# Gate matrices of a 512-token PEER layer: three parts instead of two, products one step behind, candidate sums on ScalarE

## The chip, the cores and the metric

The kernel runs on one core of one Trainium2 chip. The metric is the device time of one execution in microseconds (us): the median of the runs before is 2933.96 us. The engines are called as in the profile: PE is TensorE, DVE is VectorE, ACT is ScalarE, POOL is GpSimd, SP is SyncE, which here issues the plain loads.

## What is computed

The program runs two transformer blocks over 512 tokens of width 1024. The change touches the last stage alone, the PEER layer of the second block, cut here to what matters (8 heads, 128 keys per half, 16 kept):

```python
q = (ht @ peer_wq).reshape(T, PEER_HEADS, PEER_DK)
s1 = jnp.einsum("thd,hnd->thn", q[..., :half], peer_k1)
s2 = jnp.einsum("thd,hnd->thn", q[..., half:], peer_k2)
v1, i1 = lax.top_k(s1, PEER_TOPK)
v2, i2 = lax.top_k(s2, PEER_TOPK)
cand = v1[..., :, None] + v2[..., None, :]        # 16 x 16 sums
sc, pos = lax.top_k(cand, PEER_TOPK)
experts = e1 * PEER_NKEYS + e2                    # of 16384
gates = jax.nn.softmax(sc, axis=-1)
a = jax.nn.gelu(jnp.einsum("ckd,cd->ck", peer_u[experts], h)) * gates
out = jnp.einsum("ck,ckd->cd", a, peer_v[experts])
```

Each token so uses 128 of 16384 rows of peer_u and of peer_v.

## The kernel before, in words

All of it stands in the function peer (lines 1462 to 1903). The scores are made in four passes over peer_wq (lines 1641 to 1666), whose weights are split on ACT and POOL for PE (`split`, line 83: the fp32r copy hi). `halves` takes the top 16 of each half on DVE; `best` (line 1541) takes four heads of 128 tokens: it makes the 50 sums of pairs that can be among the 16 largest into the tile cd (lines 1553 to 1557, nine additions on DVE over four heads at once), takes the top 16 of each head (lines 1558 to 1567), and turns positions into expert numbers with one-hots. It is called eight times. Four calls for the first 256 tokens lie in the passes; four for the last 256 tokens are drawn from the generator `picks`, a piece at a time, beside the tiles below. cd and most of its neighbours have one buffer each.

The first 256 tokens are done by **gathering**. `dots` (line 1786) gathers for each of 128 choices the peer_u rows of 128 tokens by an indirect DMA from POOL (line 1784) and takes the dot product with the token on DVE (line 1791): 128 for the first 128 tokens, then 128 for the next. When 128 are done, `factors` makes the gelus; `v_sum` (line 1805) takes four gathered peer_v tiles at a time through PE (line 1812), 16 matmuls: a row product, R0 to R31 for the first 128 tokens and R32 to R63 for the next. The peer_u gathers of the second 128 tokens lie between R0 and R31, four per row product. All gathers share twelve buffers (line 1781), so a gather waits until a dot or a row product has freed one.

The last 256 tokens are done **densely**. `u_tile` (U0 to U127 below) multiplies 128 experts by the 256 tokens on PE (line 1726, 16 matmul records a tile) and ACT writes the gelu into a slot of big (line 1728), which has 96 slots. `gates` builds the matrix of gate values from one-hots: for a batch of 8 tokens DVE makes the one-hot o2 of the lower expert digit (128 wide), the one-hot eq of the upper digit for the tiles n0 to n1 of a part, and its product with the gate in two halves, og (lines 1742 to 1748); PE multiplies them (line 1752, 16 fp16 matmuls of as many columns as the part has tiles: one product, G below), and DVE multiplies the result into big (line 1756). 32 batches make a part. `v_tile` (V0 to V127) then multiplies slot n by its peer_v tile (line 1763).

The order of the work is a list written by hand (lines 1861 to 1867): U0 to U95, V0, U96, V1, U97 and so on to U127, V32, then V33 to V127. Batches G are drawn beside these steps at an even rate: the first part (64 tiles) after U63 until V0 and the second (64 tiles) after U127 until V64. `fill` (line 1850) draws gathers: after each step as many units as its rate says, 1.4 until V0 and 2.4 from then on (line 1898), where a dot counts 1 and four peer_v rows count 4. A scheduler then sets each engine's order, and engines work their own queue strictly in that order. PSUM tiles come in three groups: pu (two buffers, U tiles and the second part's products), pw (four, the first part's products until V0, then the sums of the V tiles), pr (two, row products).

Of the kernel before, what the change touches and what calls it, by code (L numbers as in the profile page):

```python
# [31 lines left out]
class Kern:  # L32
# [1430 lines left out]
    def peer(self):  # L1463
# [2 lines left out]
        act = nc.scalar.activation  # L1466
        GT, DT, DW = (0, 1), (2, 3), 256
        NS, NA = 96, 52
        parts = [0, 64, 128]
        first = dict(zip([p - 1 for p in parts[1:]], parts))  # L1470
        TB = 8
        GS = 32768.0
        with ExitStack() as ctx:
# [68 lines left out]
            def best(t, h0):  # L1542

                H = slice(h0, h0 + NH)
                xf = wk.tile([128, NH, 2, 16], F16, tag="xf", name=self.nm("xf"))
                nc.vector.tensor_copy(xf[:], ix[t][:, H])

                xe = wk.tile([128, 2, 16, NH, 16], F16, tag="xe", name=self.nm("xe"))
                for i in range(2):
                    act(xe[:, i], xf[:, :, i, :].rearrange("p h v -> p v h")[:, :, :, None].to_broadcast([128, 16, NH, 16]),  # L1550
                        AF.Copy)
                cd = wk.tile([128, NH, NC], F32, tag="cd", name=self.nm("cd"))
                o, s = 0, v[t][:, H]
                for i, n in enumerate(pairs):
                    tt(cd[:, :, o:o + n], s[:, :, 1, 0:n], s[:, :, 0, i:i + 1].to_broadcast([128, NH, n]), op=OP.add)
                    o += n
                tt(cd[:, :, o:o + 8], s[:, :, 0, 8:16], s[:, :, 1, 0:1].to_broadcast([128, NH, 8]), op=OP.add)
                pi = wk.tile([128, NH, 16], U32, tag="pi", name=self.nm("pi"))
                for i in range(NH):
                    h = h0 + i  # L1560
                    r = wk.tile([128, NC], F32, tag="mr2", name=self.nm("mr2"), bufs=2)
                    nc.vector.max(sc[t][:, h, 0:8], cd[:, i, :])
                    nc.vector.match_replace(r[:], sc[t][:, h, 0:8], cd[:, i, :], -3e38)
                    nc.vector.max(sc[t][:, h, 8:16], r[:])
                    nc.vector.max_index(pi[:, i, 0:8], sc[t][:, h, 0:8], cd[:, i, :])
                    nc.vector.max_index(pi[:, i, 8:16], sc[t][:, h, 8:16], r[:])
                yield

                pf = wk.tile([128, SL], F16, tag="pf", name=self.nm("pf"))
                nc.vector.tensor_copy(pf[:], flat(pi[:]))  # L1570
                cm = wk.tile([128, 2, 7, SL], F16, tag="cm", name=self.nm("cm"))
                cs = wk.tile([128, 2, 3, SL], F16, tag="cs", name=self.nm("cs"))
                ij = wk.tile([128, 2, SL], F16, tag="ij", name=self.nm("ij"))
                mx = wk.tile([128, SL], F16, tag="mx", name=self.nm("mx"))
                tt(cm[:, 0], cut[:, 0], pf[:, None, :].to_broadcast([128, 7, SL]), op=OP.is_le)
                tt(cm[:, 1], cm[:, 0], cut[:, 1], op=OP.mult)
                ts(mx[:], pf[:], -41.0, 0.0, op0=OP.add, op1=OP.max)
                tt(cs[:], cm[:, :, 0:3], cm[:, :, 3:6], op=OP.add)
                tt(cs[:, :, 0], cs[:, :, 0], cm[:, :, 6], op=OP.add)
                tt(cs[:, :, 1], cs[:, :, 1], cs[:, :, 2], op=OP.add)  # L1580
                tt(cs[:, :, 0], cs[:, :, 0], cs[:, :, 1], op=OP.add)
                tt(ij[:, 0], cs[:, 0, 0], mx[:], op=OP.add)
                tt(mx[:], pf[:], cs[:, 1, 0], op=OP.subtract)
                stt(ij[:, 1], pf[:], 42.0, mx[:], op0=OP.is_lt, op1=OP.mult)

                oh = wk.tile([128, 2, 16, SL], F16, tag="oh", name=self.nm("oh"))
                for i in range(2):
                    tt(oh[:, i], i16[:], ij[:, i, None, :].to_broadcast([128, 16, SL]), op=OP.is_equal)
                tt(oh[:], oh[:], xe[:].rearrange("p a v h k -> p a v (h k)"), op=OP.mult)
                for w in (8, 4, 2):  # L1590
                    tt(oh[:, :, 0:w], oh[:, :, 0:w], oh[:, :, w:2 * w], op=OP.add)
                e = e12[t][:, :, H, :].rearrange("p a h k -> p a (h k)")
                tt(e, oh[:, :, 0], oh[:, :, 1], op=OP.add)
                if t in GT:
                    stt(e[:, 0], e[:, 0], 128.0, e[:, 1], op0=OP.mult, op1=OP.add)
                    nc.vector.tensor_copy(ei[t][:, 16 * h0:16 * h0 + SL], e[:, 0])
# [134 lines left out]
            def gates(n0, n1, psum):  # L1731


                w, g = n1 - n0, TB // 2

                def by2(x, t0, w):
                    return x[:, t0:t0 + TB].rearrange("p (g i) -> p g i", i=2)[:, :, None, :].to_broadcast([128, g, w, 2])

                for t0 in range(0, DW, TB):
                    o2 = ga.tile([128, g, 128, 2], F16, tag="o2", name=self.nm("o2"), bufs=2)  # L1740
                    eq = ga.tile([128, g, w, 2], F16, tag="eq", name=self.nm("eq"))
                    tt(o2[:], io[:, None].to_broadcast([128, g, 128, 2]), by2(e2b, t0, 128), op=OP.is_equal)
                    tt(eq[:], io[:, None, n0:n1].to_broadcast([128, g, w, 2]), by2(e1b, t0, w), op=OP.is_equal)
                    og = []
                    for j in range(2):
                        o = ga.tile([128, g, w, 2], F16, tag=f"og{j}", name=self.nm("og"), bufs=2)
                        tt(o[:], eq[:], by2(gp[j], t0, w), op=OP.mult)
                        og.append(o)
                    p = psum([128, TB, w])
                    for i in range(TB):  # L1750
                        for j in range(2):
                            nc.tensor.matmul(p[:, i, :], o2[:, i // 2, :, i % 2], og[j][:, i // 2, :, i % 2], start=j == 0,
                                             stop=j == 1)
                    for n, m, b, i in slots(n0, n1):
                        b = b[:, i:i + m - n, t0:t0 + TB]
                        stt(b, p[:, :, n - n0:m - n0].rearrange("p t n -> p n t"), 1.0 / GS, b, op0=OP.mult, op1=OP.mult)  # L1756
                    yield

            def v_tile(n, acc):
                raw = load(A["peer_v_2"][n * 128:n * 128 + 128, :], [D])  # L1760
# [90 lines left out]
            def fill(n):  # L1851
                with tc.issue_after(self.pace.ins):
                    while n > 0:
                        k = next(units, None)
                        if k is None:
                            return 0.0
                        n -= k
                return n
# [4 lines left out]
            for n in range(128):  # L1863
                while u < 128 and u < n + NS:
                    seq.append(("u", u))
                    u += 1
                seq.append(("v", n))
            acc, gt, todo, room = None, None, 0, 0.0
            nbatch = DW // TB

            for j, (kind, n) in enumerate(seq):
                if kind == "v" and n == 0:
                    acc = [[pw() for _ in range(2)] for _ in range(2)]
                if kind == "v" and n in parts and gt is not None:
                    for _ in gt:
                        pass
                    gt = None
                if kind == "u":
                    if n == NA:
                        for _ in picks:  # L1880
                            pass
                        rest_of_big()
                    if n % 3:
                        next(picks, None)
                    u_tile(n)
                else:
                    v_tile(n, acc)
                if gt is not None:
                    todo += rate
                    while todo >= 1:  # L1890
                        todo -= 1
                        next(gt, None)
                if kind == "u" and n in first:
                    if gt is not None:
                        for _ in gt:
                            pass
                    gt, todo = gates(first[n], n + 1, pw if first[n] == 0 else pu), 0.0

                    rest = sum(1 for x in seq[j + 1:seq.index(("v", first[n]))])
                    rate = nbatch / max(rest - 1, 1)  # L1900

                room = fill(room + (1.4 if acc is None else 2.4))
            while next(units, None) is not None:
                pass
            for t in DT:
# [87 lines left out]
```

## Time and profile before

| | us |
|---|---|
| runs | 2929.74, 2933.96, 2935.29 |
| median of the runs | 2933.96 |
| profiled execution, device time | 2927.91 |
| profiled execution, span from first to last instruction | 2926.2 |
| busy: PE, DVE, ACT, POOL | 2709.7, 1817.2, 1020.4, 724.4 |

The span is the time between the first and last instruction of one profiled execution; some 1.7 us lie around it. A busy share is a mean over the whole program, while the stage in question runs from about 1640 us to the end, and its stretches differ. A row of the timeline gives the start, the duration, the operation with its output and inputs, and in brackets how long the engine stood idle before it and what ended the wait. A row of a group gives busy time and mean duration, and the idle time before its instructions.

### The profile page before, as it was taken

Reading aid. Unit: us, or ns where it says so; the run is one execution under the profiler, and the core shown is the slowest. Engines: PE = TensorE matmul, PEld = TensorE weight load, DVE = VectorE, ACT = ScalarE, POOL = GpSimd, SP = SyncE. Lnnn points to the kernel's source line nnn. Section 1 sums busy time; section 2 is a strip of 40 time slices with the busy share of each in tenths; the row PEclk is TensorE's granted clock in tenths of the full one; section 3 lists DMA queues with packets and bytes.
Section 4 is the critical chain, followed back from the end, with each engine's and each line's share of the span. In section 5 each row is a group of like instructions: output and inputs, shape, how many; then the busy total and the mean of one; then the engine's idle time right before and its main releaser. Section 6 shows DMA issues by size and latency. Waiting matters only on the chain.

```text
span 2926.2 us, 37189 instructions
## 1 busy us (share of the span) xinstructions
PE 2709.7 (93%) x13218; PEld 1891.9 (65%) x13218; DVE 1817.2 (62%) x3747; ACT 1020.4 (35%) x1672; POOL 724.4 (25%) x679
## 2 busy tenths in 40 slices
PE   7999969999999879999999889996999887989998
PEld 5776757777777667766778778886855443433333
DVE  5562569998888858998535399968632224761001
ACT  5442348777777653345533332210100000000000
POOL 1000050000000110101000343575045445444443
PEclk9999979999999989999999999998999888999999
DMA  7226568989999843322222347899499999999998
GB/s 259 87 84 215 208 209 323 354 320 353 350 351 347 326 146 88 102 76 69 86 91 97 119 166 276 334 409 404 159 334 371 335 349 333 335 323 405 395 383 308
DMA packets 228684, 752.03 MB, mean 257 GB/s; under 512 B 28160, under 2 KB 28448, under 8 KB 228496
## 3 DMA queue, kind: packets, MB, share of 16 engines
q1 hardware_dynamic: 145936, 458.69, 44.3%
q0 software_dynamic: 81984, 289.89, 26.9%
q8 instruction: 105, 1.72, 0.2%
q10 hardware_dynamic: 576, 1.05, 0.1%
q14 instruction: 83, 0.68, 0.1%
HBM read 736.90 MB, written 16.81 MB: 258 GB/s over the span
## 4 chain that ended last, share of the span: by engine, by line
PE 41%; DVE 8%; DMA 6%; issue 6%; POOL 3%; ACT 1%; POOLq 0%; DVEq 0%; SPq 0%; ACTq 0%
PE pw L1763 11%; PE pu L1726 6%; DMA u<-in_peer_u_dram,ei 4%; PE pm L136 4%; PE pm L138 4%; PE pm L137 4%; PE pr L1812 4%; POOL u L1784 3%; DVE u L1791 2%; PE pa L1305 2%; DMA u<-in_peer_v_dram,eT 1%; DVE cv L1236 1%; PE po L1334 1%; PE pw L138 1%; PE pw L136 1%
## 5 line engine op out<-in xcount | busy, mean ns | idle before, releaser
L84 DVE TENSOR_TENSOR lo<-raw,hi 128x1024 fp32r<-128x1024 f32 (+1 forms) x580 | 622.9, 1104 | 233.6 <-ACT hi L83 214.8
L83 ACT ACTIVATE hi<-raw 128x1024 fp32r<-128x1024 f32 (+1 forms) x600 | 557.3, 952 | 444.8 <-PE pm L137 196.5
L1791 DVE CUSTOM_DVE_ANT_0 u<-u,h 128x1024 f32<-128x1024 f32 x256 | 311.2, 1223 | 332.1 <-DMA u<-in_peer_u_dram,ei 297.8
L1763 PE MATMUL pw<-raw,big 128*128 128x512 f32 x1024 | 470.2, 607 | 1.6 <-DVE big L1756 1.6
L1726 PE MATMUL pu<-hd,raw 128*128 128x256 f32 x2048 | 464.8, 385 | 6.0 <-DVE pix L1539 3.2
L1726 PEld LDWEIGHTS pu<-hd,raw 128*128 128x128 f32 x2048 | 390.7, 193 | 79.9 <-issue 21.1
L1763 PEld LDWEIGHTS pw<-raw,big 128*128 128x128 f32 x1024 | 190.8, 193 | 255.8 <-issue 252.2
L1784 POOL DMA_INDIRECT u<-in_peer_u_dram,ei x256 | 288.6, 1127 | 263.4 <-PE pr L1812 78.0
L1784 POOL DMA_INDIRECT u<-in_peer_v_dram,eT x256 | 259.3, 1013 | 359.3 <-DVE ga L1791 224.3
L1728 ACT ACTIVATE big<-pu 128x256 f32<-128x256 f32 x128 | 49.0, 384 | 483.7 <-PE pu L1726 483.4
L137 PE MATMUL pm<-lo,xth 128*128 128x512 f32 x512 | 205.1, 401 | 6.6 <-DVE lo L84 6.6
L136 PE MATMUL pm<-hi,xth 128*128 128x512 f32 x512 | 202.2, 395 | 0.0
L138 PE MATMUL pm<-hi,xtl 128*128 128x512 f32 x512 | 201.2, 393 | 0.0
L1808 ACT ACTIVATE wz<-aT 128x4 f32<-128x4 f32 x64 | 12.8, 209 | 463.0 <-PE pr L1812 462.9
L1236 DVE SCALAR_TENSOR_TENSOR cv<-z,cols,cv 128x496 f32<-128x496 f32 (+27 forms) x240 | 166.8, 731 | 0.5
L1812 PE MATMUL pr<-u,wz 128*32 128x512 f32 x1024 | 136.9, 656 | 29.8 <-DMA u<-in_peer_v_dram,eT 29.8
L905 POOL DMA_INDIRECT yd<-y,idx x16 | 27.6, 1725 | 538.7 <-DVE y L1009 536.9
L1824 DVE TENSOR_TENSOR xe<-xe,pr 128x512 f32<-128x512 f32 x4 | 2.7, 685 | 252.1 <-PE pr L1812 247.5
L138 PE MATMUL pm<-hT,lo 128*128 128x512 f32 x384 | 151.2, 395 | 0.0
L136 PE MATMUL pm<-hT,hi 128*128 128x512 f32 x384 | 151.2, 394 | 0.0
L137 PE MATMUL pm<-hT,hi 128*128 128x512 f32 x384 | 151.0, 393 | 0.0
L137 PEld LDWEIGHTS pm<-lo,xth 128*128 128x128 f32 x512 | 96.4, 188 | 40.2 <-DVE lo L84 19.8
(575 smaller groups left out, 4302.9 us busy)
## 6 DMA issues: line engine op xcount, KB each, us to landing
raw<-in_w_gate_dram SPq DMA_DIRECT2D x128, 512.0 KB, 6.0
raw<-in_w_up_dram SPq DMA_DIRECT2D x128, 512.0 KB, 5.6
raw<-in_w_down_dram SPq DMA_DIRECT2D x128, 512.0 KB, 6.5
raw<-in_peer_uT_dram SPq DMA_DIRECT2D x128, 512.0 KB, 6.7
raw<-in_peer_v_dram SPq DMA_DIRECT2D x128, 512.0 KB, 6.9
raw<-in_w_in_dram SPq DMA_DIRECT2D x104, 256.0 KB, 2.6
wa<-in_w_ada_dram SPq DMA_DIRECT2D x48, 512.0 KB, 4.7
raw<-in_w_in_dram SPq DMA_DIRECT2D x28, 512.0 KB, 4.6
```

The source lines that it names most:

```text
L83: return (self.nc.scalar.activation(hi, src, AF.Copy), (eng or self.nc.vector).tensor_tensor(lo, src, hi.bitcast(F32), op=OP.subtract))
L84: (eng or self.nc.vector).tensor_tensor(lo, src, hi.bitcast(F32), op=OP.subtract))
L136: mm(ps, a[0], b[0], start=first, stop=False, **kw)
L137: mm(ps, a[0], b[1], start=False, stop=False, **kw)
L138: return mm(ps, a[1], b[0], start=False, stop=last, **kw)
L1236: stt(a[:, d:], z[:, :512 - d], self.col("conv_w", k * 31 + j), a[:, d:], op0=OP.mult, op1=OP.add)
L1305: nc.tensor.matmul(sc[:, :N], qT[hp][pr, i * 128:N], kT[hp][pr, :N], start=True, stop=False, skip_group_check=True)
L1726: self.u_last = nc.tensor.matmul(p[:, :DW], raw[:, k, :], hd[k // 4][:, k % 4, :], start=k == 0, stop=k == KD - 1)
L1763: self.pace = nc.tensor.matmul(acc[t][c][:], a[:, t * 128:t * 128 + 128], raw[:, c * 512:c * 512 + 512], start=n == 0, stop=n == 127)
L1784: nc.gpsimd.indirect_dma_start(out=u[:], out_offset=None, in_=A[src], in_offset=bass.IndirectOffsetOnAxis(ap=idx, axis=0))
L1791: nc.vector.tensor_tensor_reduce(u[:], u[:], h3[t][:], scale=1.0, scalar=0.0, op0=OP.mult, op1=OP.add, accum_out=ga_t[t][:, s:s + 1])
L1812: m = nc.tensor.matmul(acc[c][32 * g:32 * g + 32, :], w[:, g, 31 - r:63 - r], us[g][:, c * 512:c * 512 + 512], start=r == 0, stop=r == 31, ...
```

## The change

The gate matrix is made in three parts, of tiles 0 to 15, 16 to 79 and 80 to 127. The first is drawn from U52 until V0, the second from V0 until V16, the third from U127 until V80. In `gates` a yield stands now between the one-hots and their product, so that a batch's product is issued one draw behind its one-hots, after the tile named pace. The first part's products use pw, the others pu. The rate of `fill` before V0 is 1.5 instead of 1.4. In `best` the nine additions on DVE, each over four heads, become 36 operations on ACT, each for one head, with the first score as the bias column.

```diff
--- before.py
+++ after.py
@@ -1466,8 +1466,7 @@
         act = nc.scalar.activation
         GT, DT, DW = (0, 1), (2, 3), 256
         NS, NA = 96, 52
-        parts = [0, 64, 128]
-        first = dict(zip([p - 1 for p in parts[1:]], parts))
+        parts = [0, 16, 80, 128]
         TB = 8
         GS = 32768.0
         with ExitStack() as ctx:
@@ -1550,11 +1549,13 @@
                     act(xe[:, i], xf[:, :, i, :].rearrange("p h v -> p v h")[:, :, :, None].to_broadcast([128, 16, NH, 16]),
                         AF.Copy)
                 cd = wk.tile([128, NH, NC], F32, tag="cd", name=self.nm("cd"))
-                o, s = 0, v[t][:, H]
-                for i, n in enumerate(pairs):
-                    tt(cd[:, :, o:o + n], s[:, :, 1, 0:n], s[:, :, 0, i:i + 1].to_broadcast([128, NH, n]), op=OP.add)
-                    o += n
-                tt(cd[:, :, o:o + 8], s[:, :, 0, 8:16], s[:, :, 1, 0:1].to_broadcast([128, NH, 8]), op=OP.add)
+                s = v[t][:, H]
+                for h in range(NH):
+                    o = 0
+                    for i, n in enumerate(pairs):
+                        act(cd[:, h, o:o + n], s[:, h, 1, 0:n], AF.Identity, bias=s[:, h, 0, i:i + 1])
+                        o += n
+                    act(cd[:, h, o:o + 8], s[:, h, 0, 8:16], AF.Identity, bias=s[:, h, 1, 0:1])
                 pi = wk.tile([128, NH, 16], U32, tag="pi", name=self.nm("pi"))
                 for i in range(NH):
                     h = h0 + i
@@ -1746,15 +1747,16 @@
                         o = ga.tile([128, g, w, 2], F16, tag=f"og{j}", name=self.nm("og"), bufs=2)
                         tt(o[:], eq[:], by2(gp[j], t0, w), op=OP.mult)
                         og.append(o)
+                    yield
                     p = psum([128, TB, w])
-                    for i in range(TB):
-                        for j in range(2):
-                            nc.tensor.matmul(p[:, i, :], o2[:, i // 2, :, i % 2], og[j][:, i // 2, :, i % 2], start=j == 0,
-                                             stop=j == 1)
+                    with tc.issue_after(self.pace.ins):
+                        for i in range(TB):
+                            for j in range(2):
+                                nc.tensor.matmul(p[:, i, :], o2[:, i // 2, :, i % 2], og[j][:, i // 2, :, i % 2], start=j == 0,
+                                                 stop=j == 1)
                     for n, m, b, i in slots(n0, n1):
                         b = b[:, i:i + m - n, t0:t0 + TB]
                         stt(b, p[:, :, n - n0:m - n0].rearrange("p t n -> p n t"), 1.0 / GS, b, op0=OP.mult, op1=OP.mult)
-                    yield
 
             def v_tile(n, acc):
                 raw = load(A["peer_v_2"][n * 128:n * 128 + 128, :], [D])
@@ -1865,6 +1867,8 @@
                     seq.append(("u", u))
                     u += 1
                 seq.append(("v", n))
+
+            start = {("u", NA): 0, ("v", 0): 1, ("u", 127): 2}
             acc, gt, todo, room = None, None, 0, 0.0
             nbatch = DW // TB
 
@@ -1890,16 +1894,14 @@
                     while todo >= 1:
                         todo -= 1
                         next(gt, None)
-                if kind == "u" and n in first:
-                    if gt is not None:
-                        for _ in gt:
-                            pass
-                    gt, todo = gates(first[n], n + 1, pw if first[n] == 0 else pu), 0.0
-
-                    rest = sum(1 for x in seq[j + 1:seq.index(("v", first[n]))])
-                    rate = nbatch / max(rest - 1, 1)
-
-                room = fill(room + (1.4 if acc is None else 2.4))
+                if (kind, n) in start:
+                    i = start[kind, n]
+                    gt, todo = gates(parts[i], parts[i + 1], pu if i else pw), 0.0
+
+                    rest = seq.index(("v", parts[i])) - j - 1
+                    rate = (nbatch + 1) / (rest - 1)
+
+                room = fill(room + (1.5 if acc is None else 2.4))
             while next(units, None) is not None:
                 pass
             for t in DT:
```

The order in which the instructions stand changes in these places. On **ACT**, in the dense stage beside the later U tiles, before (big is the gelu copy of a U tile, xe a tile that best makes):

```order
L1728 ACTIVATE big<-pu_16264 128x256
L1728 ACTIVATE big<-pu_16306 128x256
L1728 ACTIVATE big<-pu_16345 128x256
L1550 ACTIVATE xe_16169<-xf_16167 128x1024 x2
L1728 ACTIVATE big<-pu_16360 128x256
L1728 ACTIVATE big<-pu_16402 128x256
```

and in the change, where the row x3 stands for three alike and the same nine follow for three more heads:

```order
L1729 ACTIVATE big<-pu_16290 128x256
L1556 ACTIVATE cd_16310<-pv_14605 128x16
L1556 ACTIVATE cd_16310<-pv_14605 128x8
L1556 ACTIVATE cd_16310<-pv_14605 128x5
L1556 ACTIVATE cd_16310<-pv_14605 128x4
L1556 ACTIVATE cd_16310<-pv_14605 128x3
L1556 ACTIVATE cd_16310<-pv_14605 128x2 x3
L1558 ACTIVATE cd_16310<-pv_14605 128x8
L1556 ACTIVATE cd_16310<-pv_14605 128x16
```

Between two gelu copies there now stand the 36 operations of one call of best. On **DVE**, at the second call of best of a pair, before (cm, cs and xf belong to the neighbouring steps of best):

```order
L1576 TENSOR_TENSOR cm_16115<-cm_16115,cut 128x448
L1546 CAST xf_16167<-pix_14609 128x128
L1578 TENSOR_TENSOR cs_16116<-cm_16115 128x384
L1555 TENSOR_TENSOR cd_16172<-pv_14605 128x4x16
L1579 TENSOR_TENSOR cs_16116<-cs_16116,cm_16115 128x2x64
L1580 TENSOR_TENSOR cs_16116<-cs_16116 128x2x64
L1555 TENSOR_TENSOR cd_16172<-pv_14605 128x4x8
L1555 TENSOR_TENSOR cd_16172<-pv_14605 128x4x5
L1581 TENSOR_TENSOR cs_16116<-cs_16116 128x2x64
L1555 TENSOR_TENSOR cd_16172<-pv_14605 128x4x4
L1555 TENSOR_TENSOR cd_16172<-pv_14605 128x4x3
```

and in the change:

```order
L1579 TENSOR_TENSOR cs_16251<-cm_16250 128x384
L1545 CAST xf_16305<-pix_14609 128x128
L1580 TENSOR_TENSOR cs_16251<-cs_16251,cm_16250 128x2x64
L1581 TENSOR_TENSOR cs_16251<-cs_16251 128x2x64
L1563 MAX sc_14641<-cd_16310 128x8
L1582 TENSOR_TENSOR cs_16251<-cs_16251 128x2x64
L1564 MATCH_REPLACE mr_3535_16348<-sc_14641,cd_16310 128x50
L1583 TENSOR_TENSOR ij_16252<-cs_16251,mx_16253 128x64
L1566 MAX_INDEX pi_16347<-sc_14641,cd_16310 128x8
```

The additions are gone from among the other small operations, and the first maximum over cd stands three rows behind xf. On **PE**, around R5 (lines 1812 and 1814), before:

```order
L1763 MATMUL pw_18769<-raw_19015,big 128x512
L1763 MATMUL pw_18770<-raw_19015,big 128x512
L1763 MATMUL pw_18771<-raw_19015,big 128x512
L1763 MATMUL pw_18772<-raw_19015,big 128x512
L1726 MATMUL pu_19030<-hd_14597,raw_19031 128x256 x4
L1726 MATMUL pu_19030<-hd_14598,raw_19031 128x256 x4
L1812 MATMUL pr_18586<-u_18992,wz_15838 32x512
L1812 MATMUL pr_18586<-u_18986,wz_15838 32x512
```

and in the change (pu tiles of line 1727 are U101, those of line 1755 products of the second part, pr is R5):

```order
L1755 MATMUL pu_19420<-og_19418,o_4152_19412 128x64
L1765 MATMUL pw_18982<-raw_19515,big 128x512
L1727 MATMUL pu_19456<-hd_14597,raw_19457 128x256 x4
L1727 MATMUL pu_19456<-hd_14598,raw_19457 128x256 x4
L1755 LDWEIGHTS o_4157_19439
L1755 MATMUL pu_19468<-og_19443,o_4157_19439 128x64
...
L1755 MATMUL pu_19468<-og_19445,o_4157_19439 128x64
L1814 MATMUL pr_18606<-u_19337,wz_15946 32x512
L1814 MATMUL pr_18606<-u_19331,wz_15946 32x512
```

Where no batch stood near R5, U101 and the products of the second part now stand ahead of R5, in PSUM tiles of the same group as U101's.

## Rows read from the trace of the kernel before

**Rows 1.** The profile's page, part 1: busy time, share of the span and instructions of each engine.

```profile
PE 2709.7 (93%) x13218; PEld 1891.9 (65%) x13218; DVE 1817.2 (62%) x3747; ACT 1020.4 (35%) x1672; POOL 724.4 (25%) x679
```

**Rows 2.** Busy time by stretch; columns: window, us, engines (instructions), PEclk, DMA share, GB/s.

```profile
1700.00:1800.00 100.00, 91.58 (x436) 78.58 (x435) 97.17 (x540) 30.27 (x45) 39.29 (x34) 0.98 0.66 228
1800.00:1860.00 60.00, 52.28 (x225) 44.78 (x225) 60.00 (x295) 11.34 (x21) 21.31 (x18) 0.93 0.81 293
1900.00:1950.00 50.00, 50.00 (x233) 44.03 (x232) 33.62 (x58) 5.78 (x15) 38.47 (x29) 1.00 1.03 409
2000.00:2050.00 50.00, 40.42 (x308) 35.09 (x309) 49.73 (x111) 3.66 (x10) 27.32 (x26) 0.84 1.01 398
2050.00:2125.00 75.00, 75.00 (x590) 65.56 (x589) 49.15 (x120) 7.70 (x23) 1.87 (x2) 1.00 0.46 155
```

**Rows 3.** Waits of 2040 to 2130: waiter, releaser, us in total, times, longest.

```profile
POOL u L1784 <- PE pr L1812: 74.1, 1, 74.1
```

**Rows 4.** Timeline of POOL; columns: start, us, line, operation [idle before <-releaser].

```profile
2127.97 0.94 POOL L1784 DMA_INDIRECT u<-in_peer_u_dram,ei  x1 [74.08 <-PE pr L1812]
...
2629.32 0.93 POOL L1784 DMA_INDIRECT u<-in_peer_u_dram,ei  x1 [0.30 <-issue]
```

**Rows 5.** Timeline of PE around the first batches and row products.

```profile
1979.38 0.64 PE L1752 MATMUL pw<-og,o 128*128 128x64 f16 x16
1979.86 3.70 PE L1726 MATMUL pu<-hd,raw 128*128 128x256 f32 x16
...
2009.46 1.29 PE L1752 MATMUL pw<-og,o 128*128 128x64 f16 x16 [21.88 <-DVE og L1747]
...
2125.79 1.92 PE L1812 MATMUL pr<-u,wz 128*32 128x512 f32 x16
...
2144.09 1.92 PE L1812 MATMUL pr<-u,wz 128*32 128x512 f32 x16
```

**Rows 6.** Groups on PE, 1900 to the end: busy, mean ns | idle before, releasers.

```profile
L1812 PE MATMUL pr<-u,wz 128*32 128x512 f32 x1024 | 136.9, 656 | 29.8 <-DMA u<-in_peer_v_dram,eT 29.8
...
L1752 PE MATMUL pu<-og,o 128*128 128x64 f16 x512 | 23.3, 196 | 30.7 <-DVE o L1742 28.3 <-DVE og L1747 1.2
```

**Rows 7.** Timeline of DVE: the 98th, 115th and last dot.

```profile
1979.73 1.23 DVE L1791 CUSTOM_DVE_ANT_0 u<-u,h 128x1024 f32<-128x1024 f32 x1 [1.01 <-DMA u<-in_peer_u_dram,ei]
...
2006.57 1.22 DVE L1791 CUSTOM_DVE_ANT_0 u<-u,h 128x1024 f32<-128x1024 f32 x1
...
2649.86 1.22 DVE L1791 CUSTOM_DVE_ANT_0 u<-u,h 128x1024 f32<-128x1024 f32 x1
```

**Rows 8.** The chain that ended last: start, us, engine and output.

```profile
2667.61 7.06 PE pw L1763 x16
...
2676.53 7.06 PE pw L1763 x16
...
2909.75 5.36 PE pw L1763 x12
```

**Rows 9.** Groups on DVE, lines 1555 and 1557 of the candidate sums.

```profile
L1555 DVE TENSOR_TENSOR cd<-pv 128x64 f32<-128x64 f32 (+3 forms) x64 | 10.1, 209 | 0.0
...
L1557 DVE TENSOR_TENSOR cd<-pv 128x32 f32<-128x32 f32 x8 | 1.5, 182 | 0.0
```

**Rows 10.** Groups on ACT: a small copy, and an operation with a bias column.

```profile
L1808 ACT ACTIVATE wz<-aT 128x4 f32<-128x4 f32 x64 | 12.8, 209 | 463.0 <-PE pr L1812 462.9
...
L203 ACT ACTIVATE rs<-ss,eps 128x1 f32<-128x1 f32 x12 | 3.5, 292 | 1.6 <-DVE ss L202 1.6
```

**Rows 11.** Groups on DVE, the batches, from 1960 to the end.

```profile
L1742 DVE TENSOR_TENSOR o<-io,e2b 128x1024 f16<-128x1024 f16 x62 | 42.2, 680 | 0.0
...
L1743 DVE TENSOR_TENSOR eq<-io,e1b 128x512 f16<-128x512 f16 x61 | 25.7, 422 | 1.1
...
L1747 DVE TENSOR_TENSOR og<-eq,gp 128x512 f16<-128x512 f16 x124 | 50.3, 418 | 27.3 <-PE pw L1752 25.9
...
L1756 DVE SCALAR_TENSOR_TENSOR big<-pw,big 128x416 f32<-128x416 f32 x32 | 18.6, 582 | 0.0
```

## Prediction, made before the changed kernel had run

> **What bounds the kernel now.** TensorE is busy for 93% of the span [rows 1], an average over stages, so I read the last stage by stretches [rows 2]. Look at the two columns PE busy and DMA share. In 1900 to 1950 TensorE and the DMA engines are both full, 409 GB/s; in 2000 to 2050 VectorE is busy for 49.7 of 50 us; in 2050 to 2125 TensorE alone is full and the DMA share falls to 0.46. Why the DMA goes slack is in POOL's waits [rows 3]: one gather waited 74.1 us for a row product. The timeline shows it: that gather goes out at 2127.97 [rows 4], right behind the first row product, R0 below, which begins at 2125.79 [rows 5]. With twelve row buffers full, nothing could be gathered before R0, and R0 stands behind U94 in TensorE's order.
>
> After R0 the gathers run as a ring on POOL: four peer_u rows, then four peer_v rows that each wait for a dot product of those four. From 2127.97 to 2629.32 [rows 4] lie 29 periods, (2629.32 - 2127.97) / 29 = **17.3 us** each, set by latency rather than by TensorE, which meanwhile waits 30.7 us for one-hots and 29.8 us for gathered rows [rows 6]. The last dot ends at 2649.86 + 1.22 = 2651.1 [rows 7]; from there TensorE works without a gap to 2909.75 + 5.36 = 2915.1 [rows 8], and 11.1 us later the span of 2926.2 ends. So the time is: when R0 restarts the ring, plus 30 periods, plus the TensorE work that the order leaves behind the last dot.
>
> **The sum, part by part.**
>
> *Candidate sums.* VectorE loses 72 additions, (64 + 8), 10.1 + 1.5 = 11.6 us [rows 9]. ScalarE gets 36 Identity operations in each of 8 calls. The nearest rows are a 128x4 scaled copy without pointer, 209 ns, and a 128x1 operation with a bias column, 292 ns [rows 10]; I take 0.25, so 36 x 0.25 = 9 us a call (7.5 to 10.5). In front of a second call's first maximum VectorE has three dots and a few small operations, some 6 us of cover, since its single buffer cd must first be read out; what is left, 1.5 to 4.5 us if a maximum waits for the whole buffer, nothing if it waits for its own head, times 4 calls, is 0 to 18 us against the 11.6 gained. The 9 us also stand ahead of gelu copies, and TensorE has two PSUM buffers, 2 x 3.45 = 6.9 us, of lead; a tile is 16 matmuls and 233 went through in 50 us [rows 2], so 3.43 to 3.45 us. Both costs fall where TensorE later waits anyway (21.88 us at G2 [rows 5]). I book +2 us for all of it, between -12 and +20.
>
> By the rows the work moves from 11.6 / 8 = 1.45 us a call on VectorE to some 9 us on ScalarE. The Trainium skill ("ScalarE: Activation LUTs", Rules for kernel authors) says that additions belong on VectorE and budgets about 0.3 us for an activation with a bias column; by it a call would take an estimated 10.8 us, 1.8 more than mine, and with 4 calls ahead of gelu copies the booked 2 us would be 9 and the sum below 2950. The row with a bias column agrees with its 0.3 us; no run here shows one at 2 to 16 columns.
>
> *First part, 16 tiles from U52 on.* At 1979.73 the 98th dot on VectorE begins [rows 7], and tiles to U66 have been loaded: 98 + 67 = 165 items of 128 x 1024 fp32, 0.524 MB, since the stage began, at 0.524 / 409 = 1.28 us each [rows 2]. The order before puts G2 behind 115 dots: it started at 2009.46 after 21.88 us [rows 5], when the 115th dot (2006.57 [rows 7]) was done; 17 dots and 4 tiles in 26.8 us are again 1.28 us each. After the change the first product that needs all 128 dots is G9 at U67: 128 dots and some 72 tiles, 200 items, (200 - 165) x 1.28 = 45 us, 2024.5, and with the 2 us above **2026.5**. VectorE's load is lighter there: a batch of 64 takes 0.68 + 0.42 + 2 x 0.42 + 0.58 = 2.5 us and a narrow second multiply [rows 11], one of 16 about 1.4 (o2 unchanged, the rest at a quarter of the columns near 0.2), so it is no longer the bound as in 2000 to 2050.
>
> From U67, R0 is 21 tiles and 18 batches away: a batch takes 0.48 us (1979.38 to 1979.86 [rows 5]), and as its 16 matmuls stay 16 I keep 0.48 for 16 columns; if the time went with the columns it would be 0.12, and R0 6.5 us earlier. 2026.5 + 21 x 3.45 + 18 x 0.48 = **2107.6**, against 2125.8: 18.2 us earlier (5 to 32). The Trainium skill ("TensorE: Matmul & The Clock Gate", Wait — 56ns, not 53.3ns?) gives small matmuls a floor of about 25 ns from start to start; by it a batch would take an estimated 0.40 us, R0 would come 1.4 us sooner and the end with it. 1979.86 - 1979.38 is 30 ns a matmul [rows 5], so the trace stands a little above that floor.
>
> *Second part, beside U96 to U111 and V0 to V15.* Before, these steps held no batches. Now 33 fall into nine ring periods. TensorE's work there is 33 tiles x 3.5 + 9 row products x 1.9 + 33 x 0.48 = 148 us, 16.5 a period, under 17.3 but close. Three places delay the ring: R1 comes 5 tiles, 4 batches and a row product after R0, 21 us, instead of 18.3 (2144.09 - 2125.79 [rows 5]): 2.5 us. U98 and U101 now share two PSUM buffers with the batches, so U101 waits for the dots of the gathers just issued and R5 stands behind U101 and a product: 3.5 + 0.5 + 1.9 us, of which 1.2 were there anyway, so 5; R3 and R6 lose 1.5 each. Together 10.5 us (0 to 15).
>
> *Third part, 48 tiles over 46 steps.* Before, with 64-wide batches over 32 steps, TensorE waited 30.7 us for one-hots [rows 6], yet that stretch is inside the mean of 17.3 [rows 4]. A thinner load and the step in hand give 3 us at most (0 to 4). The yield and the pacing cost nothing by themselves: og has two buffers, and R products never wait for them.
>
> So the ring ends S = 18.2 - 10.5 + 3 = **10.7 us** earlier.
>
> *What is left behind the last dot.* This part speaks against the change. Before, R31 stood behind V70, leaving 57 V tiles and 32 row products. Now R31 stands behind V66 and batch G86: 61 V tiles, 33 row products, 9 batches. Two V tiles take 7.06 us, and the row product between them 2676.53 - 2667.61 - 7.06 = 1.86 [rows 8]. So 61 x 3.53 + 33 x 1.86 + 9 x 0.48 = 281.0 us, behind 2.5 us for G86's one-hots and product. The end is 2651.1 + 2.5 + 281.0 + 11.1 - S = 2945.7 - S = **2935.0**; the change breaks even at S = 19.5.
>
> The profiled execution took 2927.91 us for a span of 2926.2, and the median of the runs is 2933.96, a factor of 1.0021: (2935.0 + 1.7) x 1.0021 = **2943 us**, 9 more than before.
>
> **Rivals.**
>
> *No difference.* The ring keeps nearly all of R0's lead: S near 19.5, 2934 us, and 2928 to 2940 for S from 25 down to 14. For it: the ring's mean period holds across the 64-wide batches beside V32 to V63. Against it: 16.5 of 17.3 us is little room, and U101 is in TensorE's order. 0.25.
>
> *Faster.* VectorE is full in 1800 to 1860 [rows 2]; if the 11.6 us taken from it bring every later gather forward (12 us), with no loss at R5 (10.5 back), S = 18.2 + 2 + 12 - 2.5 + 3 = 33, end 2913, 2920 us. It decides from S = 25. If the waits of TensorE were the bound instead, 21.9 + 30.7 us would go and 32 batches x 0.48 come: -37, 2897; the 29.8 us that row products wait for rows [rows 6] speak against that. 0.27 together.
>
> *Slower by the sums.* If an operation takes 0.29 us, a call blocks ScalarE for 10.5 us. Four calls stand ahead of the fp32r copies of wq that feed TensorE and cost it up to 42 us; four stand ahead of gelu copies and cost 10.5 - 6.9 = 3.6 each, 14. That is 56 us, and U67 on TensorE's own account comes at about 1991 (U65 at 1979.86 [rows 5], two tiles and 8 batches on), 35 us before the dots allow it. Beyond 35 us the delay goes on: 21 us later than forecast, S = -10, 2963 us. The trace shows ScalarE idle for most of the stage, and TensorE stalled there only 8.4 + 7.7 us in 1700 to 1860 [rows 2], so not all 42 can be direct. 0.12.
>
> That the change does not do what it says is excluded by the instruction order: batches, widths and engines are as described.
>
> **How the numbers follow.** The forecast has 0.36, for S between -5 and 14. A run of this kernel can tell about 0.2%, 5.9 us, from no change. Forecast and third rival are slower, 0.48; 0.25 no difference; 0.27 faster. The range takes S from 35 to -10: 2917 to 2964.
>
> **What would show it.** Right: POOL's long wait shrinks and its gather goes out at 2103 to 2115; 29 periods of 17.3 to 17.8 us follow; the last dot ends at 2635 to 2645; then an unbroken TensorE for about 281 us, four V tiles more than before. Wrong: R0 after 2120 (the sums, or VectorE, delay the front); periods of 17.3 through the second part (no loss at R5); TensorE idle after the last dot; or the last dot before 2626. A cd operation should be 0.19 to 0.30 us, a 16-wide batch 0.43 to 0.5.

## The result, and the profile after

The changed kernel takes **2961.4 us** (median of 5 runs, 2954.3 to 2969.6) against 2929.7 for the kernel before, measured beside it: a ratio of 1.0108, 95% interval 1.0082 to 1.0134. It is slower by 1.1%; forecast were 2943 us and slower. The profiled execution of the change is the slowest of its five, 2969.6 us with a span of 2967.9, so its rows overstate the loss by some 8 us; ratios of runs are used for every verdict, and a difference of some 8 us between two profiled executions can be the execution and not the edit.

The page, part 1, and the waits of POOL from 2117.5 to 2333.5 (for [rows 1, 3]):

```profile
PE 2734.6 (92%) x13730; PEld 1912.5 (64%) x13730; DVE 1840.6 (62%) x3835; ACT 1075.5 (36%) x1960; POOL 719.6 (24%) x679
...
POOL u L1786 <- PE pr L1814: 101.1, 8, 70.1
```

TensorE has 25 us more to do, ScalarE 55. The timelines of POOL (first gather of three groups), of TensorE (G2, R0, R1) and of VectorE (last dot), for [rows 4, 5, 7]:

```profile
2117.54 0.94 POOL L1786 DMA_INDIRECT u<-in_peer_u_dram,ei  x1 [70.14 <-PE pr L1814]
...
2333.53 0.94 POOL L1786 DMA_INDIRECT u<-in_peer_u_dram,ei  x1 [5.58 <-PE pr L1814]
...
2646.35 0.94 POOL L1786 DMA_INDIRECT u<-in_peer_u_dram,ei  x1 [0.31 <-issue]
```

```profile
1990.24 0.68 PE L1755 MATMUL pw<-og,o 128*128 128x16 f16 x16 [15.59 <-DVE o L1743]
...
2115.36 1.92 PE L1814 MATMUL pr<-u,wz 128*32 128x512 f32 x16
...
2136.53 1.92 PE L1814 MATMUL pr<-u,wz 128*32 128x512 f32 x16
```

```profile
2673.20 1.22 DVE L1793 CUSTOM_DVE_ANT_0 u<-u,h 128x1024 f32<-128x1024 f32 x1 [4.00 <-DMA u<-in_peer_u_dram,ei]
```

R0 comes 10.4 us earlier, but the next 11 ring periods take 2333.53 - 2117.54 = 216.0 us instead of 189.3, the 18 after them 312.8 (312.0 before), and the last turn, from its first gather to the end of the last dot, 28.1 instead of 21.8. So the last dot ends at 2674.4, 23.3 us later than before (-10.4 + 26.6 + 0.8 + 6.3), and behind it lie 293.5 us instead of 275.1. 23.3 + 18.4 = 41.7 us, the difference of the two spans. The same marks, read from the profiled execution of each kernel that is told of below (us):

| kernel | R0 | first 11 periods | next 18 | last dot ends | from there to the end |
|---|---|---|---|---|---|
| before | 2125.8 | 189.3 | 312.0 | 2651.1 | 275.1 |
| the change | 2115.4 | 216.0 | 312.8 | 2674.4 | 293.5 |
| e1_sums | 2141.1 | 188.2 | 314.4 | 2670.0 | 273.5 |
| e2_parts | 2098.5 | 215.5 | 313.2 | 2656.6 | 292.8 |
| e3_bank | 2110.5 | 212.3 | 303.6 | 2655.3 | 292.8 |
| e4_rate20 | 2125.4 | 178.2 | 321.7 | 2654.4 | 250.2 |
| e5_rate15 | 2102.9 | 193.6 | 311.0 | 2636.2 | 295.9 |
| e6_nostep | 2098.3 | 208.1 | 299.6 | 2631.7 | 292.9 |
| e7_parts20 | 2098.6 | 214.4 | 303.5 | 2640.7 | 267.9 |
| e8_spread | 2101.8 | 194.9 | 306.9 | 2629.7 | 303.1 |
| e9_nopace | 2094.2 | 211.9 | 306.6 | 2637.5 | 292.8 |
| e10_nostep20 | 2095.4 | 220.9 | 300.9 | 2642.2 | 272.4 |
| e11_rate18 | 2126.7 | 193.0 | 329.2 | 2673.4 | 239.6 |
| e12_after_nostep | 2110.2 | 205.6 | 295.3 | 2637.2 | 293.5 |

### The profile page after: what moved, and what is told of

Read it like the earlier page. It is cut to its first block, busy times and chain, and to the rows that moved or that the text cites. A ratio compares the mean times of both kernels' runs of the same rounds, so it can differ in the third digit from the quotient of the medians.

```text
span 2967.9 us, 38587 instructions
## 1 busy us (share of the span) xinstructions
PE 2734.6 (92%) x13730; PEld 1912.5 (64%) x13730; DVE 1840.6 (62%) x3835; ACT 1075.5 (36%) x1960; POOL 719.6 (24%) x679
## 4 chain that ended last, share of the span: by engine, by line
PE 34%; DVE 10%; DMA 9%; issue 9%; POOL 4%; ACT 1%; POOLq 0%; DVEq 0%; SPq 0%; ACTq 0%
DMA u<-in_peer_u_dram,ei 8%; PE pw L1765 8%; PE pm L136 4%; PE pm L138 4%; PE pm L137 4%; PE pu L1727 4%; POOL u L1786 3%; PE pr L1814 3%; DVE u L1793 3%; PE pa L1305 2%; DVE cv L1236 1%; PE pw L138 1%; PE pw L136 1%; PE po L1334 1%; PE pw L137 1%
## 5 line engine op out<-in xcount | busy, mean ns | idle before, releaser
L1727 PE MATMUL pu<-hd,raw 128*128 128x256 f32 x2048 | 478.4, 393 | 16.9 <-ACT big L1729 11.9
L1727 PEld LDWEIGHTS pu<-hd,raw 128*128 128x128 f32 x2048 | 398.0, 197 | 93.5 <-issue 21.3
L1814 PE MATMUL pr<-u,wz 128*32 128x512 f32 x1024 | 129.8, 626 | 11.1 <-DMA u<-in_peer_v_dram,eT 11.1
L1755 PEld LDWEIGHTS <-o 128*128 128x128 f16 x1536 | 55.9, 99 | 110.9 <-DVE o L1743 68.9
```

The lines of the kernel that those rows point to most:

```text
L1727: self.u_last = nc.tensor.matmul(p[:, :DW], raw[:, k, :], hd[k // 4][:, k % 4, :], start=k == 0, stop=k == KD - 1)
L1814: m = nc.tensor.matmul(acc[c][32 * g:32 * g + 32, :], w[:, g, 31 - r:63 - r], us[g][:, c * 512:c * 512 + 512], start=r == 0, stop=r == 31, ...
```

## Experiments: the sums and the parts apart

**e1_sums**: the nine additions replaced as in the change, all else as before (one line of each side is shown).

```diff
-tt(cd[:, :, o:o + n], s[:, :, 1, 0:n], s[:, :, 0, i:i + 1].to_broadcast([128, NH, n]), op=OP.add)
+act(cd[:, h, o:o + n], s[:, h, 1, 0:n], AF.Identity, bias=s[:, h, 0, i:i + 1])
```

> The kernel before with the candidate sums on ScalarE and nothing else. The trace of the change shows gelu copies 18 to 23 us later from the 20th tile on (1845.6 instead of 1822.3), while the 98th dot comes 6 us earlier. Theory A: the 18 us are TensorE's, and the wait of 21.9 us at G2 for the 115th dot takes them up; G2's wait shrinks to some 4 us, R0 stays at 2120 to 2128, and the time is 2925 to 2935 (before: 2930). Theory B: the sums carry through to R0; R0 at 2138 to 2146, time 2942 to 2950.

Measured 2939.6 us, 1.0045 (1.0028 to 1.0061), with R0 at 2141.1: theory B. TensorE reaches the first batch, G0, 12.4 us later (1991.8 instead of 1979.4), and G2 waits no less for that. From the waits of TensorE in e1_sums, 1640 to 2130:

```profile
PE pw L1754 <- DVE og L1749: 25.6, 1, 25.6
PE pu L1728 <- ACT big L1730: 12.3, 5, 3.8
```

The reason stands in VectorE's order: G2's one-hots are behind 115 dots in the kernel before and behind 125 here (96 in e2_parts, 107 in the change). With the sums on ScalarE the scheduler sets them back by ten or eleven dots. In e1_sums the 115th dot begins at 2009.97 and the 125th at 2022.71, and G2 begins at 2025.60; so the wait that was to take the delay up moved with it, R0 came 15.3 us later and the end followed. This is read from the traces: no run has the sums on ScalarE and the old order on VectorE. On ScalarE one call in the change (timeline, 1793 to 1800) reads:

```profile
1793.20 1.62 ACT L1556 ACTIVATE cd<-pv 128x16 f32<-128x16 f32 x8 [0.72 <-DVE pi L1566]
1794.73 0.29 ACT L1558 ACTIVATE cd<-pv 128x8 f32<-128x8 f32 x1
...
1799.84 0.28 ACT L1558 ACTIVATE cd<-pv 128x8 f32<-128x8 f32 x1
```

36 operations in 6.9 us, 0.19 each from start to start and 0.28 to 0.30 each by itself. The Trainium skill ("ScalarE: Activation LUTs", What ACT_TABLE_LOAD costs) has about 280 ns with a pointer bias, beside 0.83 ns a column, and an overlap of about 93 ns back to back: the trace agrees with both.

**e2_parts**: the change with the additions back on VectorE (e1's lines the other way).

> The change with the candidate sums back on VectorE: three parts, the step in hand and the rate of 1.5 stay. Theory A: R0's lead in the change was cut from 18 to 10 us by the sums, so here R0 comes at 2100 to 2108 instead of 2115; the second part still loses some 25 us and the work behind the last dot is the same 293 us: 2949 to 2956. Theory B: the sums were no loss, or a gain, since VectorE needs the 11.6 us: 2960 to 2970.

Measured 2947.6 us, 1.0066 (1.0041 to 1.0091): theory A, just below its 2949 and 2100, with R0 at 2098.5, 16.9 us before that of the change. So some 0.42 to 0.45% of the change's 1.08% are the sums, by this run and by e1. The product G9, which the prediction took for the one that waits for all 128 dots, begins here at 2008.43, behind 117 dots, and does not wait. TensorE meets the dots four tiles later and by way of ScalarE, whose gelu of the 128 dots (`factors`) stands ahead of gelu copies of U tiles. ScalarE, then U71 on TensorE:

```profile
2024.98 0.31 ACT L1796 ACTIVATE ga<-ga 128x128 f32<-128x128 f32 x1 [12.02 <-DVE ga L1791]
...
2025.62 10.23 PE L1725 MATMUL pu<-hd,raw 128*128 128x256 f32 x32 [1.24 <-ACT big L1727]
```

In the change TensorE comes to G9 only at 2028.09, after G2's 15.6 us, when the 128th dot is done (2023.2).

## Experiments: the second part

**e3_bank**: U96 to U127 in a PSUM tile of their own.

```diff
-                p = pu()
+                if n < NS:
+                    p = pu()
+                else:
+                    if n == NS:
+                        self.ub = pu([128, 2, DW])
+                    p = self.ub[:, n % 2, :]
```

> The change, but U96 to U127 write the two halves of one PSUM tile of their own, so that the products of the second and third part no longer alternate with U tiles in the two pu buffers. In the change eleven ring periods of the second part take 216 us instead of 189. Theory PSUM: U98 to U112 wait for dots through the shared buffers, and row products stand behind them; without it the periods fall to 17.3 to 17.8 and the time by 18 to 27 us, to 2935 to 2943. Theory load: TensorE has 16.5 of 17.3 us to do in a period, and the one-hots delay the dots on VectorE; the periods stay at 19 or more and the time at 2955 to 2965.

Measured 2951.6 us, 1.0092 (1.0070 to 1.0114), which overlaps the change and lies between the two theories. The 11 periods fell by 3.7 us of the 26.6 lost: theory load, on this point. Why the next 18 fell by 9 us no run shows.

**e8_spread**: e2_parts with parts of 48, 48 and 32 tiles, the third from V48.

```diff
-        parts = [0, 16, 80, 128]
+        parts = [0, 48, 96, 128]
-            start = {("u", NA): 0, ("v", 0): 1, ("u", 127): 2}
+            start = {("u", NA): 0, ("v", 0): 1, ("v", 48): 2}
```

> The change with the sums on VectorE and parts 0 to 47, 48 to 95 and 96 to 127, the third begun at V48: the second part's 33 batches now lie over 78 steps instead of 30. Theory load, that the batches in the stretch of U96 to U112 are what makes TensorE late with the row products there (the waits of POOL for row products rose from 3 to 31 us): periods fall from 19.6 to 17.3 to 18.3, R0 stays at 2098 to 2110, the time is 2925 to 2940. Theory order, that it is the place of the row products in the order and not the batches: periods stay at 19 or more, 2945 to 2955.

Measured 2934.5 us, 1.0028 (1.0018 to 1.0039): theory load. The 11 periods take 194.9 us, 17.7 each, 20.6 less than in e2_parts: 17 products lie in them instead of 37, and the second part's are 48 instead of 64 tiles wide, so number and width are not told apart. The waits of POOL in that stretch in e8_spread, against 101.1 in the change:

```profile
POOL u L1784 <- PE pr L1812: 72.5, 5, 54.2
```

Beyond the first long one these are 18.3 us, 31.0 in the change and 76.8 - 74.1 = 2.7 before. The first two of the 11 periods stay long: 45.6 us, as in the change (44.1) and against 33.8 before; e5_rate15, with the old two parts, has 46.4, so they come with the earlier R0 and not with the second part's batches (in the second of them V0 waits 3.9 us for VectorE's multiply in the change). The gain of e8 lies in the nine periods after them, 149.4 us instead of 170.1.

**e5_rate15**: the kernel before with the first rate alone.

```diff
-room = fill(room + (1.4 if acc is None else 2.4))
+room = fill(room + (1.5 if acc is None else 2.4))
```

> The kernel before with 1.5 instead of 1.4 units drawn per step before V0; nothing else. If the rate alone moves R0 forward in TensorE's order (from behind U94 to behind U88), R0 comes 15 to 25 us earlier, at 2101 to 2111, the ring keeps 17.3 us a period as no batches lie in it until V32, R31 leaves 4 V tiles (14 us) more behind the last dot: 2912 to 2922. Rival, that the wider batches behind U63 hold R0 back as before: 2123 to 2131.

Measured 2932.4 us, 1.0019 (1.0008 to 1.0031): neither the 2912 to 2922 nor the rival's late R0. R0 came 22.9 us earlier, as expected, without any thin first part; the last dot 14.9 earlier; and the work behind it grew by 20.8, more than the 14 expected, since 63 V tiles lie there instead of 57. An earlier R0 is taken back by the order behind it. G2 begins as before [rows 5], in TensorE's timeline:

```profile
2009.93 0.81 PE L1752 MATMUL pw<-og,o 128*128 128x64 f16 x7 [22.09 <-DVE o L1742]
```

R0 is earlier because six U tiles and six products fewer stand between G2 and R0, 6 x 3.45 + 6 x 0.48 = 23.6 us. e2_parts, with three parts and the same rate, has R0 only 4.4 us before that.

## Experiments: the step in hand

**e6_nostep**: e2_parts with each product right behind its own one-hots, and nbatch instead of nbatch + 1 draws for a part (not shown below). **e9_nopace**: e2_parts with the step but without the pacing. **e12_after_nostep**: the change with e6's edit.

```diff
                         og.append(o)
-                    yield
                     p = psum([128, TB, w])
-                    with tc.issue_after(self.pace.ins):
...
                         stt(b, p[:, :, n - n0:m - n0].rearrange("p t n -> p n t"), 1.0 / GS, b, op0=OP.mult, op1=OP.mult)
+                    yield
```

> The change with the sums on VectorE (2947.6 us) and without the step in hand: a batch's product follows its own one-hots, as before. If the step in hand and its pacing pay, TensorE waits longer for one-hots in the second and third part: 2953 to 2965. If they cost nothing and bring nothing: 2944 to 2951. If they are what delays the row products in the second part (periods of 19.6 us): 2925 to 2940.

> The change with the sums on VectorE and with the step in hand, but its products no longer issued after the tile named pace. It parts the two halves of what the kernel without the step left out (that one: 2928.3 us, with both: 2947.6). If the draw that puts a batch's one-hots a step early is what costs, because they then stand between the dots of a group on VectorE and hold up POOL's next peer_v gathers (20.5 us of such waits in the third part, 6.5 without the step): 2940 to 2953. If the pacing is what costs: 2924 to 2933.

> The change as it is, sums on ScalarE, without the step in hand alone. If sums and step are separate costs: the change less 19 us, 2938 to 2948. If the step costs only where the front is not held up by the sums: 2955 to 2965.

e6_nostep took 2928.3 us, 0.9997 (0.9984 to 1.0009), in the range of its last case, though the periods that this case blamed stay at 208.1 / 11 = 18.9 us; e9_nopace 2945.2, 1.0065 (1.0048 to 1.0083), as e2_parts; e12_after_nostep 2938.5, 1.0043 (1.0031 to 1.0056). So the draw that makes one-hots a step early costs 0.65 to 0.7%, 19 us, with sums on either engine, and the pacing nothing. The table shows where: from e2_parts to e6_nostep the first 11 periods get shorter by 7.5 us, the next 18 by 13.6, and the last turn by 3.7 (27.2 to 23.6). In VectorE's order of the 18 periods 58 batch operations (lines 1743 to 1759 in the change) stand between the first and the fourth dot of a group with the step, 29 without. Such operations delay peer_v gathers that wait for those dots. In the change, two dots of a group on VectorE, one of the operations between them, and the gather that waits behind the second:

```profile
2568.14 1.22 DVE L1793 CUSTOM_DVE_ANT_0 u<-u,h 128x1024 f32<-128x1024 f32 x1 [7.67 <-DMA u<-in_peer_u_dram,ei]
...
2570.09 0.68 DVE L1743 TENSOR_TENSOR o<-io,e2b 128x1024 f16<-128x1024 f16 x1
...
2570.96 1.21 DVE L1793 CUSTOM_DVE_ANT_0 u<-u,h 128x1024 f32<-128x1024 f32 x1
...
2572.45 1.94 POOL L1786 DMA_INDIRECT u<-in_peer_v_dram,eT  x1 [1.88 <-DVE eq L1744]
```

Waits of POOL, 2333.5 to 2680, in the change:

```profile
POOL u L1786 <- DVE eq L1744: 20.5, 12, 1.9
```

and 2308.6 to 2635 in e6_nostep (e2_parts has 20.5, as the change):

```profile
POOL u L1783 <- DVE eq L1742: 6.5, 4, 1.9
```

14.0 us less, near the 13.6 us by which e6's 18 periods are shorter than e2's. Not all fits: e9's profile, its fastest run, has the same 20.5 us and yet 306.6 us for the 18 periods, e3_bank has the 58 operations and 303.6, and the kernel before has 100 of them, no such wait, and 312.0. So the size is sure from the medians; that these waits are the cause is argued from the traces and not shown by a run.

## Experiments: the work behind the last dot

**e4_rate20** and **e11_rate18** are the kernel before, **e7_parts20** is e2_parts and **e10_nostep20** e6_nostep, with the second rate alone changed:

```diff
-room = fill(room + (1.4 if acc is None else 2.4))
+room = fill(room + (1.4 if acc is None else 2.0))
```

> The kernel before with 2.0 instead of 2.4 units drawn per step after V0; nothing else. It tests the reading that the end is R0, 30 ring periods and the TensorE work left behind the last dot. By it the ring keeps 17.3 to 18 us a period, R31 moves from behind V70 to about V90, and 20 V tiles, 70 us, leave the tail; the tail is then bound by some 165 transfers of 1.28 us, 212 us: 2875 to 2900. Rival, that TensorE's total work or the transfers bound the whole: 2925 to 2935. Rival, that later row products slow the ring to 18.5 or more: 2905 to 2925.

> The change with the sums on VectorE and 2.0 instead of 2.4 units per step after V0. By the reading that the end is R0 (2098), the ring, and what the order leaves behind the last dot: periods of 18.5 to 19.6 in the second part, where TensorE has four steps and as many batches a period, 17.3 to 18 after it; last dot 2655 to 2670; 15 to 20 V tiles fewer behind it: 2890 to 2910. Rival, that the gain of the lower rate does not add to the parts: 2925 to 2945.

> Three parts, sums on VectorE, no step in hand, 2.0 units per step after V0: the two gains together. If they add (19 us for the step, 30 for the rate at the same parts): 2895 to 2905. If the ring is bound by TensorE's steps at this rate anyway, so that only one counts: 2908 to 2920.

> The kernel before with 1.8 units per step after V0. At 2.0 it took 2905.7. Reading: at 1.8 a ring period holds 4.4 tiles, 4.4 x 3.53 + 1.9 = 17.6 us of TensorE's work, so the ring follows TensorE at 17.6 to 18.5, the last dot comes at 2660 to 2680, and the row products behind V127 are bound by their gathers, 5.1 us each: 2898 to 2912, no clear gain over 2.0. Rival, that less work behind the last dot still pays: 2880 to 2895.

e4_rate20 took **2905.7 us, 0.9923 (0.9900 to 0.9945)**, the best of all; e7_parts20 2917.9, 0.9967 (0.9955 to 0.9978); e10_nostep20 2918.4, 0.9976 (0.9963 to 0.9990); e11_rate18 2914.7, 0.9961 (0.9946 to 0.9975). In e4 the ring's 29 periods take 499.9 us, 501.4 before, and 36 V tiles instead of 57 lie behind the last dot, 250.2 us instead of 275.1: the reading holds in kind. The gain is less than forecast (2875 to 2900), because the end then belongs to gathers; TensorE's timeline in e4_rate20:

```profile
2855.42 3.64 PE L1812 MATMUL pr<-u,wz 128*32 128x512 f32 x16 [2.22 <-DMA u<-in_peer_v_dram,eT]
2860.54 3.64 PE L1812 MATMUL pr<-u,wz 128*32 128x512 f32 x16 [1.48 <-DMA u<-in_peer_v_dram,eT]
2865.65 1.93 PE L1812 MATMUL pr<-u,wz 128*32 128x512 f32 x16 [1.48 <-DMA u<-in_peer_v_dram,eT]
```

a row product every 5.1 us with no V tile left to lay between. At 2.0 the step in hand no longer costs (e7 and e10 agree), and the three parts with the rate of 1.5 are worse than the old two: only one of the two gains counts, as e10 expected, while e7 lies between its two ranges. At 1.8 the time is just above the 2898 to 2912 expected: the periods alternate between 15.8 and 18 to 22 us, the last dot comes at 2673.4, and TensorE is busy for 520.3 of the 521.2 us from 2128.8 to 2650, so it bounds the ring there. (A period's work by the expectation's terms is 4.4 x 3.53 + 1.9 = 17.4 us, not 17.6.)

## Why the prediction was right, and where its terms were off

Slower was right, and by the reading forecast for it. The size was not: 9 us were forecast, some 32 came, and the terms missed in both directions. The last dot was to come 10.7 us earlier and came 23.3 later, beyond the -10 that the range was made from, and 2961.4 lies above the forecast's own band (S from -5 to 14, up to 2959) and next to the third rival's 2963. That it lies inside 2917 to 2964 is luck in part: the upper bound is 1.0102 of the median before that it was made from, 2933.96, and the measured ratio is 1.0108. (By the same sum S = 35 gives 2918.5, not 2917.) Of the four signs of being right one came, the TensorE work behind the last dot; the first gather went out at 2117.5 and not by 2115, the 29 periods were 18.2 us and not up to 17.8, and the last dot ended at 2674.4 and not by 2645.

- **The reading** of the end as R0, ring and what is left behind was right: every row of the table adds up by it, with the last turn of 21.8 to 28.1 us, and e4 moves the far end of it alone. The term behind the last dot was 281.0 + 2.5 + 11.1 = 294.6, measured 293.5: the change's one loss that was sized right, and what made the forecast slower. The 6.3 us more of the last turn in the change stand in no term.
- **"I book +2 us for all of it"** failed: the sums cost 14 us (e1: +0.45%; e12 against e6 the same). The bound of +20 held it. The size of a call was 6.9 us, not 9; what failed was the cover: by the traces the wait at G2 does not take up a delay when the order moves G2's one-hots behind ten more dots. The third rival had TensorE held up by the calls, which is what e1 shows, but with 56 us ahead of U67 and 35 us of cover; measured were 12.4 us ahead of G0 and no cover.
- **"The yield and the pacing cost nothing by themselves"** failed for the yield: 19 us. I looked at buffers and products, and not at which dots the one-hots come to stand between on VectorE. The 3 us booked as a gain for the third part became 0.8 us of loss; without the step the 18 periods gain 12 to 17.
- **"Together 10.5 us" in the second part** was 26.6. The place I named, U101 and its PSUM buffers, carries only some 4 (e3); fewer and narrower batches there take 20.6 back (e8). R1's period lost 2.9 us (2.5 forecast) and R5's 6.7 (5 forecast), but R2's lost 7.5, R8's 6.4 and R11's 4.4, which the list did not have. My count of 16.5 us of TensorE's work in a period of 17.3 was under. By stretch, in the change and before (columns as in [rows 2]):

```profile
2117.50:2333.50 216.00, 194.91 (x1267) 124.69 (x1267) 135.23 (x305) 11.15 (x35) 85.05 (x88) 0.91 0.86 309
2128.00:2317.30 189.30, 180.04 (x735) 105.14 (x734) 56.97 (x95) 11.11 (x35) 91.18 (x88) 0.97 0.96 357
```

  TensorE was busy for 17.7 us a period, 16.4 before without batches, at a granted clock of 0.91 (0.97 before), a mean between its two levels of 1.2 and 2.4 GHz. In the change's stretch it waited 11.4 us for one-hots and 7.4 for the multiplies of VectorE.
- **The first part** was near in its time, by another path. The 128 dots were done at 2024.9 (e2) and 2023.2 (the change), near the 2024.5 forecast, but G9 waited for them in neither. Without the sums R0 was forecast at 2105.6 and came at 2098.5 (e2), as TensorE met the dots at U71 and not at U67; with the sums the forecast was 2107.6 and R0 came at 2115.4, behind a wait of 15.6 us at G2 that the sum did not have. So two errors partly cancel in R0. Most of the lead is the rate's: 23 us by e5 alone, 27 by e2. A 16-wide batch took 0.41 to 0.47 us, near the 0.48 kept.

Taken apart: the parts and the rate 0.9997 (e6), the step +0.7%, the sums +0.45%; together 1.011, as measured.

## What to carry to other kernels

A wait covers a delay only if the order behind it stays: look up what the scheduler puts in front of the waiting instruction after the change, too. Where a loop is bound by latency, look at the operations that come to stand between its links on each engine, and not at the busy time alone. And look at what an earlier start leaves behind the loop's last turn: here a lower rate of drawing, which lays more of the other work inside the loop, gave 0.8% that no earlier start gave.

## What the runs showed that was not expected

VectorE loses 11.6 us of additions and the kernel gets slower by 14 us from that edit alone, with VectorE full around it [rows 2]. And a pipelining step that is meant to save TensorE's waits made them longer. In the third part TensorE waits 38.2 us for the one-hots o2 in e2_parts and 26.5 in e6_nostep, without the step.
